# A two-layer hybrid decoder trunk: the prologue's modulation blocks in halves, its rotary sines moved behind its last split, and the last norm turned token-major by TensorE

## The chip, the cores and the metric

The kernel runs on one core of one Trainium2 chip. The metric is the time of one execution on the device in microseconds (us), the median of several runs. Three runs of the kernel before gave 935.73, 937.77 and 939.75 us.

## The reference

Two layers over 256 tokens of width 1024, in float32. Each layer forms six modulation vectors from the conditioning vector `c`, runs three attention branches side by side from one input projection, and then an MLP. Only the start and the end matter here:

```python
c_act = jax.nn.silu(c)
for l in range(DEPTH):
    mod = c_act @ w_ada[l] + b_ada[l]                 # w_ada[l]: 1024 x 6144
    shift1, scale1, gate1, shift2, scale2, gate2 = jnp.split(mod, 6, axis=-1)
    hdn = modulate(rmsnorm(x, norm1_g[l]), shift1, scale1)
    proj = hdn @ w_in[l]
    q_lat, c_kv, k_pe, sb_qkv, mb_qkv, gates = jnp.split(proj, SPLIT_POINTS, axis=-1)
    ...                                               # MLA, stick-breaking and MoBA attention
    x = x + gate1[:, None, :] * (merged @ w_out[l])
    hdn = modulate(rmsnorm(x, norm2_g[l]), shift2, scale2)
    x = x + gate2[:, None, :] * (jnp.square(jax.nn.relu(hdn @ w_ff1[l])) @ w_ff2[l])
return rmsnorm(x, final_norm_g)
```

`rmsnorm` divides by the root of the mean square over the 1024 channels, `modulate` is `h * (1 + scale) + shift`. The rotary embeddings of two branches need sines and cosines of the positions.

## The kernel before

The residual `x` lies with channels on the partitions: 8 tiles `x[:, k, :]` of 128 channels by 256 tokens. Weights are streamed in blocks of 1 MB by DMAs that SyncE (SP) issues. A block is a `Job`: `fetch` loads it into a tile `ws`, ScalarE (ACT) rounds it into `wh` and VectorE (DVE) forms the remainder `wl = ws - wh` (`split_piece`, four pieces to a job), and TensorE (PE) multiplies with three matmuls per product (`wh` by high part, `wh` by low part, `wl` by high part). The jobs stand in one list and are worked through in order.

The prologue is written out by hand and keeps its order on every engine. It computes `mod` of the first norm on DVE: `ada` multiplies a block of `w_ada` (two columns of 1024 numbers per partition) with the broadcast activated `c` in `cb` and sums along the row. Channel pairs q = 0 to 3 follow each other. For each pair, block 4 + q (the scale) and block q (the shift) are loaded as `adaw`, and then two jobs of the input projection (`ws`, jobs 2q and 2q + 1, cut into pieces of 256 KB). The pair's two channel tiles are scaled (`ht`) and shifted. For q = 0 and 1 TensorE multiplies them unsplit in float32 (`hf` by `ws`, "plain" jobs 0 to 3); for q = 2 and 3 they are split into `hh`, `hl` (tile `act`) and their weights (jobs 4 to 7) into `wh`, `wl`. All four pairs add up in the same PSUM banks (`first`). When the last pair is through, ACT copies the banks out to `sbqk`, from which the stick-breaking scores `z` are made; the `z` tiles take the same PSUM slots as the banks (tag "at", two slots). Then follow job 8 (tile `ps`, of the MoBA projection), jobs 9 and 10, and job 11, a further block of `w_ada`.

SP's queue holds DMAs back by semaphores: each waits for the one issued eight before it, and later ones for the `ws` slot that they fill (three slots).

`table_angles` reduces the rotary angles on DVE and `tables` takes their absolute value and sines on ACT, which loads another function table and loads the old one back. `warm` issues matmuls that nobody reads.

At the end, `x_last` adds the last two channel tiles, `Rms.sum` adds the squares over channels on PE, `Rms.root` forms the reciprocal root for a 128 x 256 tile, and four DVE products make the output, still with channels on the partitions, in four DMAs.

Of the kernel before, what the change touches and what calls it, by code (L numbers as in the profile page):

```python
# [20 lines left out]
D = 1024  # L21
# [14 lines left out]
WARM = 12, 2, 20  # L36
# [4 lines left out]
def trunk(ctx, tc, xT, heads, pos, signs, masks, gfin, wada, win, wkpe, wuq, wukv, wo, wout, wff1, wff2, out):  # L41
# [56 lines left out]
    def table_angles():  # L98
        row = t256("row")
        nc.vector.tensor_copy(row[0:1, :], posi)  # L100
        posf = mmps("posf")[:, 0, :]
        nc.tensor.matmul(posf, minus[0:1, :], row[0:1, :], start=True, stop=True)
        c1 = 6.28125
# [7 lines left out]
        nc.vector.tensor_scalar(n, n, MAGIC, None, op0=OP.subtract)  # L111
        for f in (c1, c2, c3):
            nc.vector.scalar_tensor_tensor(ang, n, -f, ang, op0=OP.mult, op1=OP.add)
        nc.vector.tensor_scalar(ang, ang, PI_SAFE, -PI_SAFE, op0=OP.min, op1=OP.max)

# [23 lines left out]
    class Job:  # L139
        def __init__(self, src, f, parts, raw=False, plain=None, mms=24):  # L140
            self.src, self.f, self.parts, self.raw, self.plain, self.mms = src, f, parts, raw, plain, mms

# [276 lines left out]
    def first_jobs(qk_done, sbv, start):  # L419
# [12 lines left out]
        def part(u, i, o, q):  # L432
            def go(wh, wl):
                ps = bank(u)
                ks = range(2 * q, 2 * q + 2)
# [11 lines left out]
                else:  # L447
                    v_part(ps, i, wh, wl, o, ks, q < PLAIN_Q)
# [8 lines left out]
        for q in range(4):  # L457
            for us, tag in ((range(4), "wh"), (range(4, 6), "wl")):
                jobs.append(Job([win[0, u][:, q * 512:q * 512 + 512] for u in us], 512 * len(us),
                                [part(u, i, 512 * (u - us[0]), q) for u in us for i in range(2)],  # L460
                                plain=tag if q < PLAIN_Q else None))
# [126 lines left out]
    def layer(l):  # L588
# [244 lines left out]
        def x_last(i, ps, sec):  # L833
# [5 lines left out]
            if i == 0:  # L839
                go()  # L840
            else:
                rms["last"] = go
# [19 lines left out]
        def seam(then, n):  # L862
            def go():
                drain()
                tc.no_sync_barrier()
                with tc.manual_schedule():
# [3 lines left out]
                    else:  # L870
                        rms["last"]()
                        rms["q"].sum()
                        r = rms["q"].root()
                        for u in range(4):
                            o = t512("out")
                            nc.vector.tensor_mul(o, rms["xg"][:, 2 * u:2 * u + 2, :], bc(r))
                            nc.sync.dma_start(out[:, 2 * u:2 * u + 2, :], o)
                tc.no_sync_barrier()
                rest()
            return go  # L880

# [106 lines left out]
    with tc.manual_schedule():  # L988
# [19 lines left out]
        fetch_to(6)  # L1008
# [21 lines left out]
        table_angles()  # L1030
        warm(WARM[1])
        rq = Rms(D)
        for u in range(4):
# [3 lines left out]
        ada(0, 4, first_ada[4])  # L1037
        gs0 = gain(0, 48, 1, (0, 2))
        r = rq.root(scalar=True)
        nc.gpsimd.dma_start(csr, signs)  # L1040
        hf.append(work.tile([128, 4, S], F32, name="hf", tag="v", bufs=2))

        def start_job(i):
            split_to(i, PIECES)
            for part in jobs[i].parts:
                part(jobs[i].wh, jobs[i].wl)
# [6 lines left out]
        for q in range(4):  # L1053
            ks = range(2 * q, 2 * q + 2)
            if q:
                ada(0, 4 + q, first_ada[4 + q])
                gain(0, 48, 1, (2 * q, 2 * q + 2), gs0)
            if q < PLAIN_Q:
                ts = [scaled(k) for k in ks]
                ada(0, q, first_ada[q])  # L1060
                for k, t in zip(ks, ts):
                    nc.scalar.activation(hf[0][:, k, :], t, AF.Identity, bias=col(0, 0, k))
            else:
                ada(0, q, first_ada[q])
                if q < 3:
                    split_to(2 * q, 1)
                modulate(0, r, gs0, 0, ks)
            if q < 3:
                start_job(2 * q)
                start_job(2 * q + 1)  # L1070
                if q == 0:
                    tables()
                if q == 2:
                    fetch_to(7)
        split_to(6, PIECES)
        split_to(7, PIECES)
        for k in range(2 * PLAIN_Q):
            split(hh[:, k, :], hl[:, k, :], hf[0][:, k, :])
        state["auto"] = True
        fetch_to(7 + WS)  # L1080
# [99 lines left out]
```

## Time and profile before

| | before |
|---|---|
| median of 3 runs | 937.77 us (935.73 to 939.75) |
| profiled execution, its own time | 938.25 us |
| span in the profile | 936.5 us, 19142 instructions |
| PE busy | 915.7 us (98%) |
| DVE busy | 730.5 us (78%) |
| ACT busy | 599.1 us (64%) |
| DMA, mean over the span | 223 GB/s |
| granted TensorE clock, mean | 0.995 |

The span is the time between the first and the last thing that the profiler saw on the core; the execution's own time is 1.75 us longer. A PE that is busy 98% of the span leaves some 20 us in which it waits, and those lie in the first 90 us, at two places in the middle and behind the last matmul. PE's busy time is modelled, so the waits are better read from when an instruction starts than from the sum.

### The profile page before, as it was taken

How to read it: one execution, taken by the hardware profiler on the slowest of the kernel's cores; microseconds unless marked ns; L12 is line 12 of the kernel's file. 1: busy time of each engine (PE TensorE's matmuls, PEld its weight loads, DVE VectorE, ACT ScalarE, POOL GpSimd, SP SyncE). 2: the span in 40 equal slices, each digit the busy share in tenths (PEclk: the TensorE clock that was granted, in tenths of full speed). 3: DMA queues.
4: the chain of work that ended last, by engine and by line, in shares of the span. 5: the costliest groups of instructions: out<-in, count | busy, mean ns of one | idle time of the engine just before them, and what ended most of it. 6: DMA issues, size and time to landing. Idle time of an engine off the chain costs nothing.

```text
span 936.5 us, 19142 instructions
## 1 busy us (share of the span) xinstructions
PE 915.7 (98%) x7771; PEld 889.6 (95%) x7772; DVE 730.5 (78%) x1414; ACT 599.1 (64%) x1251; POOL 9.6 (1%) x15
## 2 busy tenths in 40 slices
PE   7998999999999999999999999999999999999996
PEld 4998999899999999999999999989999999999995
DVE  6878788887799976767897978879787989554554
ACT  4277678867576874645576677886677677563641
POOL 0000000000000000000000000000000000000012
PEclk9999999999999999999999999999999999999998
DMA  9956564565657388677847554645666647755531
GB/s 339 386 205 231 185 225 159 214 235 196 245 225 270 140 310 305 236 270 266 324 174 274 222 203 155 229 169 210 240 221 228 212 150 284 256 181 190 186 121 45
DMA packets 32634, 208.77 MB, mean 223 GB/s; under 512 B 3745, under 2 KB 4130, under 8 KB 8994
## 3 DMA queue, kind: packets, MB, share of 16 engines
q1 hardware_dynamic: 32400, 207.35, 61.7%
q8 instruction: 61, 1.00, 0.4%
q0 software_dynamic: 144, 0.20, 0.1%
q14 instruction: 27, 0.22, 0.1%
q10 hardware_dynamic: 2, 0.00, 0.0%
HBM read 206.49 MB, written 1.05 MB: 222 GB/s over the span
## 4 chain that ended last, share of the span: by engine, by line
PE 84%; DVE 6%; DMA 6%; ACT 2%; issue 1%; SPq 0%; DVEq 0%; ACTq 0%
PE ps L342 17%; PE ps L343 16%; PE ps L344 16%; PE ff L939 5%; PE ff L942 5%; PE ff L940 5%; DMA ws<-win 5%; PE pre L364 4%; DVE wl L178 3%; PE po L469 1%; DMA ws<-wada 1%; PE vps L342 1%; PE vps L344 1%; PE vps L343 1%; PE s L524 1%; PE z L510 1%
## 5 line engine op out<-in xcount | busy, mean ns | idle before, releaser
L178 DVE TENSOR_TENSOR wl<-ws,wh 128x512 fp32r<-128x512 f32 (+1 forms) x592 | 378.7, 675 | 128.6 <-ACT wh L177 128.0
L177 ACT ACTIVATE wh<-ws 128x512 fp32r<-128x512 f32 (+1 forms) x592 | 336.8, 615 | 208.2 <-PE ps L343 97.3
L342 PE MATMUL ps<-act,wh 128*128 128x256 f32 x1120 | 312.0, 279 | 0.0
L344 PE MATMUL ps<-act,wl 128*128 128x256 f32 x1120 | 310.3, 277 | 0.0
L343 PE MATMUL ps<-act,wh 128*128 128x256 f32 x1120 | 310.1, 277 | 0.0
L342 PEld LDWEIGHTS ps<-act,wh 128*128 128x128 f32 x1120 | 210.4, 188 | 0.5 <-DVE wl L178 0.3
L344 PEld LDWEIGHTS ps<-act,wl 128*128 128x128 f32 x1120 | 210.9, 188 | 0.0
L343 PEld LDWEIGHTS ps<-act,wh 128*128 128x128 f32 x1120 | 210.4, 188 | 0.2
L939 PE MATMUL ff<-fh,wh 128*128 128x256 f32 x448 | 123.6, 276 | 0.0
L940 PE MATMUL ff<-fl,wh 128*128 128x256 f32 x448 | 123.6, 276 | 0.0
L942 PE MATMUL ff<-fh,wl 128*128 128x256 f32 x448 | 123.6, 276 | 0.0
L242 DVE SCALAR_TENSOR_TENSOR ws<-ws,cb 128x1024 f32<-128x1024 f32 x80 | 95.9, 1221 | 22.5 <-DMA ws<-wada 22.1
L939 PEld LDWEIGHTS ff<-fh,wh 128*128 128x128 f32 x448 | 84.1, 188 | 0.0
L940 PEld LDWEIGHTS ff<-fl,wh 128*128 128x128 f32 x448 | 84.1, 188 | 0.0
L942 PEld LDWEIGHTS ff<-fh,wl 128*128 128x128 f32 x448 | 84.1, 188 | 0.0
L544 ACT ACTIVATE e<-s,st 128x128 f32<-128x128 f32 (+1 forms) x64 | 26.0, 432 | 23.6 <-DVE st L539 23.6
L364 PE MATMUL pre<-xh,wh 128*128 128x258 f32 x96 | 28.3, 295 | 0.0
L364 PE MATMUL pre<-xh,wl 128*128 128x258 f32 x96 | 27.1, 283 | 0.0
L364 PE MATMUL pre<-xl,wh 128*128 128x258 f32 x96 | 27.1, 282 | 0.0
L342 PE MATMUL vps<-wh,act 128*128 128x256 f32 x96 | 26.9, 280 | 0.0
L343 PE MATMUL vps<-wl,act 128*128 128x256 f32 x96 | 26.7, 278 | 0.0
L344 PE MATMUL vps<-wh,act 128*128 128x256 f32 x96 | 26.7, 278 | 0.0
(259 smaller groups left out, 1738.6 us busy)
## 6 DMA issues: line engine op xcount, KB each, us to landing
ws<-wff SPq DMA_DIRECT2D x64, 1024.0 KB, 4.9
ws<-win SPq DMA_DIRECT2D x50, 1024.0 KB, 4.9
ws<-wada SPq DMA_DIRECT2D x40, 1024.0 KB, 4.9
ws<-wo SPq DMA_DIRECT2D x12, 1024.0 KB, 4.9
adaw<-wada SPq DMA_DIRECT2D x8, 1024.0 KB, 9.2
ws<-wout SPq DMA_DIRECT2D x8, 1024.0 KB, 4.9
ws<-win SPq DMA_DIRECT2D x24, 256.0 KB, 9.1
ws<-wuq SPq DMA_DIRECT2D x6, 768.0 KB, 4.3
```

The costliest lines, as they stand in the source:

```text
L177: nc.scalar.activation(job.wh[:, a], job.ws[:, a], AF.Copy)
L178: nc.vector.tensor_sub(job.wl[:, a], job.ws[:, a], job.wh[:, a].bitcast(F32))
L242: nc.vector.scalar_tensor_tensor(w, w, 1.0, cb, op0=OP.mult, op1=OP.mult, accum_out=mods[l][:, 2 * b + i:2 * b + i + 1])
L342: nc.tensor.matmul(o, wh, ah, start=first, stop=False)
L343: nc.tensor.matmul(o, wh, al, start=False, stop=False)
L344: nc.tensor.matmul(o, wl, ah, start=False, stop=last)
L364: nc.tensor.matmul(ps[:, i, 0:258], w[:, c:c + 128], a[:, k, :], start=k == 0 and n == 0, stop=k == KT - 1 and n == 2, skip_group_check=True)
L469: nc.tensor.matmul(po[64 * h:64 * h + 64, u, o:256], v[:, k, vc:vc + 64], pT[:, h, c:c + n], start=k == 0, stop=k == 1, tile_position=(0, ...
L544: nc.scalar.activation(e[:, h, a:b], s[:, h, a:b], AF.Exp, scale=scale, bias=st[:, 4 + c:5 + c], accum_out=st[:, 8 + c:9 + c])
L939: nc.tensor.matmul(o, wh[:, c0:c0 + 128], fh[:, k, :], start=st, stop=False, skip_group_check=True)
L940: nc.tensor.matmul(o, wh[:, c0:c0 + 128], fl[:, k, :], start=False, stop=False, skip_group_check=True)
L942: nc.tensor.matmul(o, wl[:, c0:c0 + 128], fh[:, k, :], start=False, stop=en, skip_group_check=True)
```

## The change

In the prologue each block of `w_ada` is loaded in two halves of 512 KB, in the order scale, shift, scale, shift, and each half is worked off by itself (`ada_col`: product and sum, then one 128 x 1 operation). The first two channel tiles are modulated one at a time, and the first group of matmuls goes over the channel tile k outermost. One pair of squares moves from ACT to DVE. The angles' reduction is cut in three: the position matmul stays, the first four operations stand behind the first pair's modulation, and the last four, with the sines on ACT, stand behind the last splits of the prologue. Jobs 6 and 7 load into spare slots, so that job 8 can be fetched earlier. Fewer warm matmuls are issued. In pairs 2 and 3 the first piece of the weight split stands between the two low parts of the activations.

At the end, the products with the gain are turned by TensorE transposes to tokens on the partitions, the sums of squares are made for tokens on the partitions (128 x 2), the root is taken of 128 x 2 numbers, and ACT and DVE copy the turned tiles out with the root as a scale, in three pieces each, with six DMAs.

```diff
-WARM = 12, 2, 20
+WARM = 7, 2, 14
...
     def fetch(i):
         job = jobs[i]
-        job.ws = wpool.tile([128, 2048], F32, name="ws", tag=job.plain or "ws", bufs=WB if job.plain else WS)
+        if job.spare:
+            job.ws = slot("ws").rearrange("p a b -> p (a b)")
+        else:
+            job.ws = wpool.tile([128, 2048], F32, name="ws", tag=job.plain or "ws", bufs=WB if job.plain else WS)
...
+        def tail():
+            q, xg = rms["q"], rms["xg"]
+            ft = [atps(f"ft{t}") for t in range(2)]
+            ts = mmps("tsum")
...
+            total([q.acc] + q.late, True, False)
+            q.late = []
+            turn(range(1))
+            x_one(7, rms["end"], 5)
+            q.square_late(x[:, 7, :])
+            nc.vector.tensor_scalar(xg[:, 7, :], x[:, 7, :], gf[:, 7:8], None, op0=OP.mult)
+            total(q.late, False, True)
+            turn(range(1, KT))
...
+            for a, b in ((0, 256), (256, 512), (512, 1024)):
+                h, c = a // 512, slice(a % 512, a % 512 + b - a)
+                nc.scalar.activation(os[0][h][:, c], ft[0][:, h, c], AF.Copy, scale=r[:, 0:1])
+                nc.vector.tensor_scalar(os[1][h][:, c], ft[1][:, h, c], r[:, 1:2], None, op0=OP.mult)
+                for t, e in ((0, nc.scalar if h else nc.sync), (1, nc.sync)):
+                    e.dma_start(out[toks[t], a:b], os[t][h][:, c])
...
             for b in (4 + q, q):
-                t = slot("adaw").rearrange("p a b -> p (a b)")
-                nc.sync.dma_start(t, wada[0, b])
-                first_ada[b] = t
+                first_ada[b] = slot("adaw").rearrange("p a b -> p (a b)")
+            for i in range(2):
+                for b in (4 + q, q):
+                    nc.sync.dma_start(first_ada[b][:, i * D:i * D + D], wada[0, b][:, i * D:i * D + D])
...
+        def ada_col(b, i):
+            w = first_ada[b][:, i * D:i * D + D]
+            c = slice(2 * b + i, 2 * b + i + 1)
+            m = mods[0][:, c]
+            nc.vector.scalar_tensor_tensor(w, w, 1.0, cb, op0=OP.mult, op1=OP.mult, accum_out=m)
+            if b < 4:
+                nc.vector.tensor_add(m, m, vec[:, 0, c])
+            else:
+                k = 2 * (b - 4) + i
+                nc.vector.scalar_tensor_tensor(gs0[:, k:k + 1], m, onep[:, k:k + 1], vec[:, 0, 48 + k:49 + k],
+                                               op0=OP.add, op1=OP.mult)
...
+        ada_col(4, 0)
+        ada_col(0, 0)
+        r = rq.root(scalar=True)
...
+        plain_act(0, scaled(0))
+        ada_col(4, 1)
+        ada_col(0, 1)
+        plain_act(1, scaled(1))
+        next(angles)
+        split_to(1, PIECES)
+        for k in range(2):
+            for i in range(2):
+                start_job(i, [k])
...
+        for q in (2, 3):
+            k = 2 * q
+            ada_col(4 + q, 0)
+            ada_col(q, 0)
+            ta = scaled(k)
+            high(k, ta)
+            ada_col(4 + q, 1)
+            low(k, ta)
+            ada_col(q, 1)
+            tb = scaled(k + 1)
+            high(k + 1, tb)
+            split_to(2 * q, 1)
+            low(k + 1, tb)
...
         split_to(6, PIECES)
         split_to(7, PIECES)
         for k in range(2 * PLAIN_Q):
             split(hh[:, k, :], hl[:, k, :], hf[0][:, k, :])
+        next(angles)
+        tables()
         state["auto"] = True
-        fetch_to(7 + WS)
```

What this does to the order on the engines is shown at three places. The first is ScalarE at the end of the prologue: `wh` are the rounded weights of jobs 6 and 7 (four pieces each) and then of job 8, `act<-hf` the splits of the plain activations, `sbqk<-first` the copies out of the PSUM banks. Before:

```order
L335 ACTIVATE act<-ht,mod 128x256 x2
L177 ACTIVATE wh<-ws 128x512 x4
L177 ACTIVATE wh<-ws 128x256 x4
L234 ACTIVATE act<-hf 128x256 x4
L177 ACTIVATE wh<-ws 128x512 x4
L596 ACTIVATE sbqk<-first 128x256
```

The same place in the changed kernel, where `tab` is the tile of the rotary tables:

```order
L184 ACTIVATE wh<-ws 128x512 x4
L184 ACTIVATE wh<-ws 128x256 x4
L241 ACTIVATE act<-hf 128x256 x4
L121 ACTIVATE tab<-tab 128x512
L122 ACT_TABLE_LOAD
L122 ACTIVATE tab<-tab 128x512
L123 ACTIVATE tab<-tab,quarter 128x512
L124 ACT_TABLE_LOAD
L184 ACTIVATE wh<-ws 128x512 x4
L603 ACTIVATE sbqk<-first 128x256
```

The five instructions on `tab`, which stood before behind the first `hf` pair, now stand between the last splits and the weights of job 8, and ahead of the copies to `sbqk`.

The second place is VectorE at the same point of the program. Before (`act<-hf` are the low parts of the plain activations, the five `wl` those of job 8 and one piece of job 9, `ws<-ws,cb` job 11's block of `w_ada`):

```order
L334 SCALAR_TENSOR_TENSOR ht<-x,gs_233,rr 128x256 x2
L338 SCALAR_TENSOR_TENSOR act<-ht,mod_90,act 128x256 x2
L178 TENSOR_TENSOR wl<-ws,wh 128x512 x4
L178 TENSOR_TENSOR wl<-ws,wh 128x256 x4
L235 TENSOR_TENSOR act<-hf,act 128x256 x4
L178 TENSOR_TENSOR wl<-ws,wh 128x512 x5
L242 SCALAR_TENSOR_TENSOR ws,mod_90<-ws,cb 128x1024 x2
```

In the changed kernel, from the last scaled tile on:

```order
L1107 SCALAR_TENSOR_TENSOR ht<-x,gs_226,rr 128x256
L185 TENSOR_TENSOR wl<-ws,wh 128x512
L1117 SCALAR_TENSOR_TENSOR act<-ht,mod_90,act 128x256
L185 TENSOR_TENSOR wl<-ws,wh 128x512 x3
L185 TENSOR_TENSOR wl<-ws,wh 128x256 x4
L242 TENSOR_TENSOR act<-hf,act 128x256 x4
L115 SCALAR_TENSOR_TENSOR tab<-tab 128x512 x3
L116 TENSOR_SCALAR tab<-tab 128x512
L185 TENSOR_TENSOR wl<-ws,wh 128x512 x5
L249 SCALAR_TENSOR_TENSOR ws,mod_90<-ws,cb 128x1024
```

One piece of the weight split now stands between the two low parts of the activations, and four operations on the angles stand ahead of job 8's pieces.

The third place is VectorE at the first channel pair, from the position's cast on. Before:

```order
L100 CAST row<-posi 1x256
L109 TENSOR_SCALAR tab<-posf,head 128x256 x2
L110 TENSOR_SCALAR tab<-tab 128x512
L111 TENSOR_SCALAR tab<-tab 128x512
L113 SCALAR_TENSOR_TENSOR tab<-tab 128x512 x3
L114 TENSOR_SCALAR tab<-tab 128x512
L242 SCALAR_TENSOR_TENSOR adaw,mod_90<-adaw,cb 128x1024 x2
L247 TENSOR_TENSOR mod_90<-mod_90,head 128x2
L325 SCALAR_TENSOR_TENSOR gs_233<-mod_90,head 128x2
L313 TENSOR_TENSOR v<-v,y_237 128x256
L315 SCALAR_TENSOR_TENSOR rr<-v,yh 128x256
L1050 SCALAR_TENSOR_TENSOR ht<-x,gs_233,rr 128x256 x2
```

In the changed kernel:

```order
L100 CAST row<-posi 1x256
L1083 TENSOR_TENSOR sq<-x 128x256 x2
L1084 TENSOR_TENSOR sq<-sq 128x256
L1097 SCALAR_TENSOR_TENSOR adaw,mod_90<-adaw,cb 128x1024
L1102 SCALAR_TENSOR_TENSOR gs_226<-mod_90,onep,head 128x1
L1097 SCALAR_TENSOR_TENSOR adaw,mod_90<-adaw,cb 128x1024
L1099 TENSOR_TENSOR mod_90<-mod_90,head 128x1
L320 TENSOR_TENSOR v<-v,y_233 128x256
L322 SCALAR_TENSOR_TENSOR rr<-v,yh 128x256
L1107 SCALAR_TENSOR_TENSOR ht<-x,gs_226,rr 128x256
```

All work on the angles left the front of the first block, two squares came to VectorE, and the first scaled tile needs two halves in place of a whole block.

## Rows read from the trace of the kernel before

**Rows 1.** Waits of PE: who waited for whom, us in total, times, longest.

```profile
PE first L441 <- ACT hf L1062: 3.1, 1, 3.1
```

**Rows 2.** Stretches: busy us per engine (instructions), granted clock, DMA share, GB/s.

```profile
25.00:30.00 5.00, 5.00 (x25) 4.41 (x24) 1.70 (x5) 0.91 (x2) 0.00 (x0) 1.00 1.00 412
```

**Rows 3.** DVE's timeline: start, length (us), line, operation, idle before.

```profile
30.05 1.23 DVE L242 SCALAR_TENSOR_TENSOR adaw<-adaw,cb 128x1024 f32<-128x1024 f32 x1 [3.32 <-DMA adaw<-wada]
...
32.74 1.22 DVE L242 SCALAR_TENSOR_TENSOR adaw<-adaw,cb 128x1024 f32<-128x1024 f32 x1
...
47.18 0.89 DVE L338 SCALAR_TENSOR_TENSOR act<-ht,mod,act 128x256 fp32r<-128x256 f32 x2 [0.18 <-ACT act L335]
48.10 3.84 DVE L178 TENSOR_TENSOR wl<-ws,wh 128x512 fp32r<-128x512 f32 x8
51.86 1.42 DVE L235 TENSOR_TENSOR act<-hf,act 128x256 fp32r<-128x256 f32 x4
53.20 2.49 DVE L178 TENSOR_TENSOR wl<-ws,wh 128x512 fp32r<-128x512 f32 x4
```

**Rows 4.** ACT's timeline at the end of the prologue.

```profile
50.76 1.33 ACT L234 ACTIVATE act<-hf 128x256 fp32r<-128x256 f32 x4
51.99 2.19 ACT L177 ACTIVATE wh<-ws 128x512 fp32r<-128x512 f32 x4
54.08 0.37 ACT L596 ACTIVATE sbqk<-first 128x256 f32<-128x256 f32 x1
```

**Rows 5.** DVE's timeline on the rotary angles.

```profile
10.12 2.15 DVE L113 SCALAR_TENSOR_TENSOR tab<-tab 128x512 f32<-128x512 f32 x3
12.30 0.43 DVE L114 TENSOR_SCALAR tab<-tab 128x512 f32<-128x512 f32 x1
```

**Rows 6.** ACT's timeline on the rotary sines: the first and the last of five.

```profile
20.52 0.61 ACT L118 ACTIVATE tab<-tab 128x512 f32<-128x512 f32 x1
...
23.70 1.28 ACT L121 ACT_TABLE_LOAD   x1
```

**Rows 7.** PE's timeline from the first scores to job 8.

```profile
57.84 0.70 PE L478 MATMUL z<-sbqk 64*128 64x256 f32 x4
...
58.60 0.60 PE L478 MATMUL z<-sbqk 64*128 64x256 f32 x4
...
59.79 0.36 PE L342 MATMUL ps<-act,wh 128*128 128x256 f32 x1
```

**Rows 8.** Stretches behind the prologue and behind one wait of layer 1.

```profile
70.00:75.00 5.00, 3.98 (x35) 3.76 (x34) 2.98 (x5) 4.62 (x8) 0.00 (x0) 1.00 0.92 360
75.00:80.00 5.00, 3.75 (x25) 3.31 (x24) 5.00 (x9) 5.00 (x11) 0.00 (x0) 1.00 0.15 31
85.00:90.00 5.00, 4.36 (x42) 3.96 (x40) 4.96 (x11) 2.00 (x4) 0.00 (x0) 1.00 0.87 326
619.00:623.00 4.00, 4.00 (x15) 3.21 (x14) 1.82 (x5) 2.85 (x7) 0.00 (x0) 0.57 0.61 188
```

**Rows 9.** DVE's timeline at job 11's block of `w_ada` and behind it.

```profile
62.77 1.22 DVE L242 SCALAR_TENSOR_TENSOR ws<-ws,cb 128x1024 f32<-128x1024 f32 x1 [5.87 <-DMA ws<-wada]
...
69.36 0.95 DVE L500 SCALAR_TENSOR_TENSOR l<-z,l 128x768 f32<-128x768 f32 x1
```

**Rows 10.** Issues of DMAs of the whole span: count, size, median us to landing.

```profile
ws<-wada SPq DMA_DIRECT2D x40, 1024.0 KB, 4.9
```

**Rows 11.** Timeline of the end, all engines.

```profile
926.36 0.48 DVE L799 SCALAR_TENSOR_TENSOR x<-xl,mod,x 128x256 f32<-128x256 f32 x1 [2.24 <-PE xl L942]
...
927.34 0.70 PE L299 MATMUL ssum<-sql,negs 128*128 128x256 f32 x2 [0.16 <-ACT sql L291]
...
930.55 2.50 DVE L876 TENSOR_TENSOR out<-xg,rr 128x512 f32<-128x512 f32 x4
931.26 2.14 SPq L877 DMA_DIRECT2D outT<-out  x4
```

**Rows 12.** PE's timeline at one group of transposes.

```profile
137.96 1.48 PE L560 MATMUL pt<-head,e 128*128 128x128 f32 x12
```

More of the change, by code (lines that the diff above doesn't have):

```diff
@@ L841, in x_last @@
             else:
-                rms["last"] = go
+                rms["last"], rms["end"] = go, ps
         def wout_done(u):
@@ L870, in go @@
                     else:
[L871 to L877, printed above, removed]
+                        tail()
                 tc.no_sync_barrier()
@@ L1007, in trunk @@
         ada_fetch(3)
-        fetch_to(6)
+        fetch_to(8)
         nc.sync.dma_start(msk, masks)
@@ L1029, in trunk @@
             nc.scalar.activation(cb[:, 512 * h:512 * h + 512], cps[:, h, :], AF.Copy)
-        table_angles()
+        onep = cpool.tile([128, KT], F32, name="onep")
+        nc.vector.tensor_scalar(onep, vec[:, 0, 8:16], 1.0, None, op0=OP.add)
+        angles = table_angles()
+        next(angles)
         warm(WARM[1])
         rq = Rms(D)
-        for u in range(4):
+        sqa = t512("sq")
+        for k in range(2):
+            nc.vector.tensor_mul(sqa[:, k, :], x[:, k, :], x[:, k, :])
+        nc.vector.tensor_add(sqa[:, 0, :], sqa[:, 0, :], sqa[:, 1, :])
+        rq.late.append(sqa[:, 0, :])
+        for u in range(1, 4):
             rq.square(*x_pair(u), keep=True)
@@ L1036, in trunk @@
         warm(WARM[2])
[L1037 to L1046, printed above, removed]
+        gs0 = cpool.tile([128, KT], F32, name="gs00")
+        first_ht = {}
+        def ada_col(b, i):
[9 more added lines that the diff above has]
+                                               op0=OP.add, op1=OP.mult)
         def scaled(k):
@@ L1051, in scaled, with plain_act @@
             return t
[L1053 to L1074, printed above, removed]
+        def plain_act(k, t):
+            nc.scalar.activation(hf[0][:, k, :], t, AF.Identity, bias=col(0, 0, k))
@@ new lines, in high, with low, start_job @@
+        def high(k, t):
+            nc.scalar.activation(hh[:, k, :], t, AF.Identity, bias=col(0, 0, k))
+        def low(k, t):
+            nc.vector.scalar_tensor_tensor(hl[:, k, :], t, col(0, 0, k), hh[:, k, :].bitcast(F32),
+                                           op0=OP.add, op1=OP.subtract)
+        def start_job(i, ks=None):
+            split_to(i, PIECES)
+            for part in jobs[i].parts:
+                part(jobs[i].wh, jobs[i].wl, ks)
+        ada_col(4, 0)
+        ada_col(0, 0)
@@ new lines, in trunk @@
+        r = rq.root(scalar=True)
+        nc.gpsimd.dma_start(csr, signs)
+        hf.append(work.tile([128, 4, S], F32, name="hf", tag="v", bufs=2))
+        plain_act(0, scaled(0))
[4 more added lines that the diff above has]
+        split_to(1, PIECES)
+        for k in range(2):
+            for i in range(2):
+                start_job(i, [k])
+        for i in range(2):
+            ada_col(5, i)
+            ada_col(1, i)
+            plain_act(2 + i, scaled(2 + i))
@@ new lines, in trunk @@
+        start_job(2)
+        start_job(3)
+        for q in (2, 3):
[11 more added lines that the diff above has]
+            low(k + 1, tb)
+            if q == 2:
+                for i in (4, 5):
+                    start_job(i)
+                    fetch_to(i + 5)
@@ L1078, in trunk @@
             split(hh[:, k, :], hl[:, k, :], hf[0][:, k, :])
+        next(angles)
+        tables()
         state["auto"] = True
-        fetch_to(7 + WS)
     tc.no_sync_barrier()
```

40 lines of the change are left out of this document (32 added, 8 removed).

## The prediction, on record before the changed kernel ran

> **What bounds the kernel now.** I read first who TensorE waits for, then what the stretches move, then the timelines of VectorE and ScalarE at the places found.
>
> TensorE's one long wait in the prologue is 3.1 us, for the first modulated tile [rows 1]. That invites an earlier start, and most of the change works on it. But an earlier first matmul pays only if what follows also comes earlier. From 25 to 30 us the 16 DMA engines are busy all the time at 412 GB/s, while VectorE works 1.70 of 5 us [rows 2]. VectorE then stands 3.32 us until block 6 of the modulation weights lands at 30.05 [rows 3]. So the third channel pair is paced by the stream of weights, and no reordering ahead of it makes that block land earlier; its first half can come earlier by half a block.
>
> Behind 30.05 VectorE is full to the end of the prologue: the two activation splits start at 47.18, the weight splits of jobs 6 and 7 at 48.10, the low parts of the plain activations at 51.86, job 8's split at 53.20, with a wait of 0.18 us among them [rows 3]. ScalarE ends its last prologue work at 51.99, rounds job 8's weights and copies the banks out from 54.08 on [rows 4]. TensorE takes the first scores at 57.84, the second at 58.60, job 8 at 59.79 [rows 7]. The order that counts is therefore: VectorE's chain from block 6, then ScalarE's copies, then the scores, which share PSUM slots with the banks and stand ahead of job 8 on TensorE.
>
> **The change, step by step.** All times are those of the profiled execution, 938.25 us with a span of 936.5.
>
> Start of the third pair. Half a block is 0.52 MB, at 412 GB/s 1.27 us [rows 2]. VectorE starts at 28.78 instead of 30.05 [rows 3]. Bytes and their order up to there stay the same.
>
> What rows 2 show is a full stream, whatever the size of a transfer. The Trainium skill (DMA: Bandwidth & Descriptors, section Bandwidth) says to batch transfers to at least 1 MiB, and its fit gives each some 2 us of fixed cost; by that rule the eight more transfers would cost, as an estimate, up to 16 us if they ran one by one. The trace's full stream, with transfers of 256 KB among them, does not bear that out.
>
> VectorE on pairs 2 and 3. Each pair has four small operations where there were three, and each waits for the sum just before it. Two columns with their two small operations take 2.69 us now, 30.05 to 32.74 [rows 3]; bounds for the addition are 0 and 0.5 us per pair, I take 0.2, since most of the operations exist already. Worse, a piece of the weight split now stands between the two low parts. It needs ScalarE to pass the scaled tile (like a copy of 128 x 256, 0.37 us [rows 4]) and to round a piece (128 x 512, like the 0.61 us [rows 6]), so VectorE stands about 1.0 us where it stood 0.18: 0.8 more per pair (0 if a piece were rounded ahead; it is not, ScalarE's row order has it behind). The low parts of the plain activations thus end at 53.20 - 1.27 + 0.4 + 1.6 = 53.93.
>
> The angles. The four operations that move behind them take 10.12 to 12.73, 2.61 us [rows 5]: 56.54. Before, they lay where VectorE waited for weights anyway.
>
> The sines. ScalarE has been idle since its own splits and waits for the angles. The block runs from 20.52 to 24.98, 4.46 us [rows 6]: 61.0. It stood where ScalarE had nothing to do; now job 8's weights and the copies out of the banks queue behind it. Three passes of about 0.6 and two table loads of 1.28 us fill these 4.46 us [rows 6]. The Trainium skill (ScalarE: Activation LUTs, section What ACT_TABLE_LOAD costs) puts a switch at 2.66 us, half of it a drain; by that the block would cost, as an estimate, 2.8 us more. The rows leave no room for a drain.
>
> Copies and scores. Job 8's four pieces take 54.08 - 51.99 = 2.09 us [rows 4]: 63.1. Four copies, one more piece, four copies follow: copies of 0.37 us overlap, so four take 1.05 to 1.5 us, I take 1.05; with a piece of 0.52 the second scores can start at 65.75, against 58.60: **+7.15 us** for TensorE. It will have stood since the end of the last pair, about 57.5, since an earlier first group cannot run ahead of the third pair's data. All that TensorE gains at the start is lost there, and so the finer first group, the moved squares and the fewer warm matmuls cost and bring nothing; their cover is this wait.
>
> What is late next. Job 11's load waits for job 8's split, which ended at 53.20 + 2.49 = 55.69 [rows 3] and now ends at about 63.95 (ScalarE's 63.1, a subtraction behind). With 4.9 us to landing [rows 10], the link being empty, VectorE gets it at 68.85 instead of 62.77, and the softplus term `l` behind it starts 6.1 us later than 69.36 [rows 9]. On that chain TensorE waits 2.27 us between 70 and 80 and 0.64 us between 85 and 90 [rows 8]. TensorE arrives 7.15 us late, the chain 6.1: about 1 us of these waits goes, and **+6.1 us** remain. Bounds: all 2.9 us of the waits absorbed, +4.3. Or the clock: after a wait the granted clock stood at a mean of 0.57 over 4 us in layer 1 [rows 8], 1.7 us lost, and a wait of six us may bring the same; if nothing absorbs it, +8.9. Behind 90 us TensorE is busy all but a few us, so what remains is not won back.
>
> The end. The last tile of `x` comes at 926.36 as before [rows 11]. The sums over tokens are four narrow matmuls behind the last square; 0.70 us is what the wide ones took [rows 11], I take 0.5: 927.85. Fourteen transposes follow, and twelve took 1.48 us in layer 0 [rows 12]; at 0.11 us each they end at 929.4. The root on 128 x 2 numbers is hidden behind them. Three copies per engine, like two pieces of 0.37 and one of 0.61 us with the PSUM read on top, take 1.5 us: 930.9, where the last product ended at 933.05 [rows 11]. Five of the six issues are SP's, at a quarter to half a us each [rows 11]: the last at 931.4 instead of 933.07, which gives 1.7 us. But the same 1.05 MB have to go out, 2.5 us at the 412 GB/s of rows 2, and from the first issue at 931.26 to the end of the span at 936.5 passed 5.24 us; from a first issue at 929.9 the same 5.24 lead to 935.1, which gives 1.4. I take **-1.3 us**; bounds 0 (transposes twice as slow) and -2.1 (all that the last copy gains).
>
> Sum: 938.25 + 6.1 - 1.3 = 943.05. The median shown is 0.5 us lower than the profiled execution and the runs spread over 4 us; I name **943.0 us**, 0.56% above the median. About 0.5%, 4.7 us, is what a measurement of this kernel can tell from no change: 933.1 to 942.5 counts as the same.
>
> **The rivals.**
>
> The early start is kept (faster). If the chain from block 6 were not what decides, TensorE would start earlier by the two columns left out (2.7 us [rows 3]) and the angles' 2.6 us [rows 5], 5.3 in all, and keep it: 938.25 - 5.3 - 1.3 = 931.7. For it speaks that TensorE's own wait list names only the first tile [rows 1]; against it the 3.32 us at 30.05 [rows 3]. It decides if ScalarE's sines are through by 52.0, where it took up job 8 before: 9 us earlier than worked out, more than that whole wait. Chance 0.11.
>
> The sines stay hidden (same). If the angles came early enough that ScalarE did them while TensorE is in the last pair, nothing moves there and the end alone counts: 936.9. It needs the block to end by 54, 7 us earlier. Or all waits to 90 us are absorbed and the end gives its best: 938.25 + 4.3 - 2.1 = 940.4. The first has a chance of 0.11; the second is the forecast's lower end.
>
> The halves slow the stream (slower). If it ran at the 360 GB/s of 70 to 75 us [rows 8] and not at 412, the 9 MB ahead of block 6's half would take 25.2 and not 22.0 us: 3.2 us more, 946.2. Rows 2 speak against it. Chance 0.05. (The Trainium skill's batching rule in DMA: Bandwidth & Descriptors, above, points this way.)
>
> **How the numbers follow.** The forecast has 0.73, its own range is 940.4 to 947.2 (8.9 and no gain at the end). Its centre lies just above the border of 942.5, so I put 0.45 above and 0.28 below it. Slower: 0.45 + 0.05 = 0.50. Same: 0.28 + 0.11 = 0.39. Faster: 0.11. A range from 937.5 to 947.0 holds the forecast but for its far end, the stream's case and part of the hidden sines, and leaves out the kept start: about 0.8.
>
> **What will show it.** In the changed profile TensorE's first group starts near 15 us, and TensorE stands for six us or so between 57 and 66 with ScalarE's copies as the releaser. VectorE's first column of block 6 starts near 28.8, the angles' last operation ends near 56.5, the second table load near 61, job 8 starts near 67. Job 11's columns start near 69. At the end the last output is issued about 5 us behind the last update of `x`. I am wrong if job 8 starts before 62, if VectorE has no wait ahead of block 6, or if the end takes as long as before.

## The result and the profile after

| | before | changed |
|---|---|---|
| median of 10 runs each, same chip | 938.64 us | 944.05 us |
| ratio, with its 95% interval | | 1.0072 (1.0051 to 1.0093) |
| profiled execution, own time / span | 938.25 / 936.5 us | 943.68 / 941.9 us |
| PE, DVE, ACT busy | 915.7, 730.5, 599.1 us | 920.3, 731.9, 599.0 us |

The ratio is estimated from all runs; the two medians alone give 1.0058. The changed kernel is slower by 0.6 to 0.7%, as forecast (943.0 us, slower as the likeliest of the three).

PE's list of waits in the changed kernel (total, times, longest) has a new head: the scores `z` wait for ScalarE's copies.

```profile
PE z L485 <- ACT sbqk L604: 5.1, 1, 5.1
PE first L448 <- ACT wh L184: 3.3, 2, 2.9
PE mvps L349 <- DVE gate L137: 3.0, 2, 1.5
```

VectorE's timeline, from block 6's first column on:

```profile
29.02 1.22 DVE L1097 SCALAR_TENSOR_TENSOR adaw<-adaw,cb 128x1024 f32<-128x1024 f32 x1 [3.34 <-DMA adaw<-wada]
...
36.89 0.69 DVE L185 TENSOR_TENSOR wl<-ws,wh 128x512 fp32r<-128x512 f32 x1 [1.09 <-ACT wh L184]
...
48.88 0.69 DVE L185 TENSOR_TENSOR wl<-ws,wh 128x512 fp32r<-128x512 f32 x1 [1.09 <-ACT wh L184]
...
53.03 1.43 DVE L242 TENSOR_TENSOR act<-hf,act 128x256 fp32r<-128x256 f32 x4
54.38 2.14 DVE L115 SCALAR_TENSOR_TENSOR tab<-tab 128x512 f32<-128x512 f32 x3
56.55 0.43 DVE L116 TENSOR_SCALAR tab<-tab 128x512 f32<-128x512 f32 x1
62.17 2.50 DVE L185 TENSOR_TENSOR wl<-ws,wh 128x512 fp32r<-128x512 f32 x4 [5.20 <-ACT wh L184]
...
69.55 1.23 DVE L249 SCALAR_TENSOR_TENSOR ws<-ws,cb 128x1024 f32<-128x1024 f32 x1 [3.52 <-DMA ws<-wada]
...
76.26 0.96 DVE L507 SCALAR_TENSOR_TENSOR l<-z,l 128x768 f32<-128x768 f32 x1
```

Against [rows 3] block 6 starts 1.03 us earlier. Two waits of 1.09 us at the split piece are new, then come the angles, then 5.20 us of standing for job 8's rounded weights. Job 11's column comes 6.78 us later than in [rows 9]. ScalarE's timeline shows what VectorE stood for:

```profile
51.54 1.32 ACT L241 ACTIVATE act<-hf 128x256 fp32r<-128x256 f32 x4
57.01 0.63 ACT L121 ACTIVATE tab<-tab 128x512 f32<-128x512 f32 x1 [4.15 <-DVE tab L116]
57.66 1.28 ACT L122 ACT_TABLE_LOAD   x1
58.95 0.63 ACT L122 ACTIVATE tab<-tab 128x512 f32<-128x512 f32 x1
...
60.22 1.28 ACT L124 ACT_TABLE_LOAD   x1
61.51 2.19 ACT L184 ACTIVATE wh<-ws 128x512 fp32r<-128x512 f32 x4
...
65.97 0.43 ACT L604 ACTIVATE sbqk<-first 128x256 f32<-128x256 f32 x1
```

ScalarE takes job 8's weights up at 61.51, where [rows 4] have 51.99: 4.15 us of waiting for the angles and 4.5 us of sines lie ahead of them. PE's timeline of the scores and job 8 (to compare with [rows 7]), then stretches with the granted clock as the last number but two:

```profile
64.84 1.23 PE L485 MATMUL z<-sbqk 64*128 64x256 f32 x4 [5.14 <-ACT sbqk L604]
...
66.46 1.22 PE L485 MATMUL z<-sbqk 64*128 64x256 f32 x4
...
68.83 0.56 PE L349 MATMUL ps<-act,wh 128*128 128x256 f32 x1
```

```profile
64.00:66.00 2.00, 1.16 (x6) 0.99 (x8) 1.33 (x3) 2.00 (x8) 0.00 (x0) 0.50 0.41 57
66.00:68.00 2.00, 2.00 (x14) 1.38 (x10) 0.03 (x1) 2.00 (x6) 0.00 (x0) 0.50 0.79 319
68.00:70.00 2.00, 2.00 (x15) 1.96 (x14) 0.45 (x1) 2.00 (x5) 0.00 (x0) 0.50 0.35 147
70.00:75.00 5.00, 5.00 (x45) 5.00 (x44) 5.00 (x10) 3.41 (x5) 0.00 (x0) 0.98 0.30 70
75.00:80.00 5.00, 5.00 (x46) 5.00 (x46) 3.14 (x5) 2.72 (x4) 0.00 (x0) 1.00 1.01 423
85.00:90.00 5.00, 5.00 (x41) 4.92 (x41) 5.00 (x10) 3.61 (x7) 0.00 (x0) 1.00 0.62 211
```

Behind its wait TensorE runs at the lower of its two levels, 1.2 GHz, to 70 us; a group of scores takes 1.23 us where it took 0.70. Job 8 is 9.04 us late, but the waits of 70 to 90 us in [rows 8] are gone. The end, all engines:

```profile
932.66 0.48 DVE L806 SCALAR_TENSOR_TENSOR x<-xl,mod,x 128x256 f32<-128x256 f32 x1 [2.24 <-PE xl L986]
...
933.65 0.61 PE L897 MATMUL tsum<-negs,sql 128*128 128x2 f32 x4
...
934.12 1.72 PE L892 MATMUL ft<-head,xg 128*128 128x128 f32 x14
...
935.88 1.54 DVE L922 TENSOR_SCALAR out<-ft,st 128x256 f32<-128x256 f32 x3 [0.43 <-PE ft L892]
936.27 2.43 SPq L924 DMA_DIRECT2D outT<-out  x5
937.22 0.37 ACTq L924 DMA_DIRECT2D outT<-out  x1
```

The last update of `x` comes 6.30 us later than in [rows 11], and from it to the end of the span pass 9.24 us instead of 10.14. The difference of the spans, 5.4 us, is 6.30 - 0.90.

### The profile page after: what moved, and what is told of

The parts are those of the page before. It is cut to its first block, busy times and chain, and to the rows that moved or that the text cites. A ratio compares the mean times of both kernels' runs of the same rounds, so it can differ in the third digit from the quotient of the medians.

```text
span 941.9 us, 19180 instructions
## 1 busy us (share of the span) xinstructions
PE 920.3 (98%) x7780; PEld 894.6 (95%) x7781; DVE 731.9 (78%) x1423; ACT 599.0 (64%) x1251; POOL 8.7 (1%) x14
## 4 chain that ended last, share of the span: by engine, by line
PE 79%; DVE 10%; DMA 5%; ACT 4%; issue 1%; SPq 0%; DVEq 0%; ACTq 0%
PE ps L349 15%; PE ps L350 15%; PE ps L351 15%; PE ff L983 5%; PE ff L984 5%; PE ff L986 5%; DVE wl L185 4%; PE pre L371 4%; DMA ws<-win 2%; DMA adaw<-wada 2%; PE po L476 1%; PE vps L349 1%; PE vps L350 1%; PE vps L351 1%; ACT wh L184 1%; DMA ws<-wada 1%
## 5 line engine op out<-in xcount | busy, mean ns | idle before, releaser
L350 PE MATMUL ps<-ml,wh 128*128 128x256 f32 x96 | 26.8, 282 | 0.6 <-DVE ml L242 0.6
L349 PE MATMUL vps<-wh,act 128*128 128x256 f32 x96 | 26.9, 280 | 0.0
L349 PE MATMUL ps<-mh,wh 128*128 128x256 f32 x96 | 26.6, 280 | 0.2 <-ACT mh L241 0.2
```

The source lines that it names most:

```text
L349: nc.tensor.matmul(o, wh, ah, start=first, stop=False)
L350: nc.tensor.matmul(o, wh, al, start=False, stop=False)
```

## Experiments

The theory: what counts is when ScalarE gets to job 8's weights, because the load of job 11 and with it VectorE's chain hang on them; TensorE's own start counts less. The rivals: the halves, the half clock, or the new end cost the time. The table has four moments of each profiled execution (us) and the timed ratio to the kernel before: TensorE's start of job 8, VectorE's first column of job 11, the first row maxima of the MoBA softmax, the last update of `x`.

| kernel | job 8 | job 11 | row maxima | last `x` | ratio (95% interval) |
|---|---|---|---|---|---|
| before | 59.79 | 62.77 | 123.00 | 926.36 | |
| changed | 68.83 | 69.55 | 130.03 | 932.66 | 1.0072 (1.0051 to 1.0093) |
| 1 before, sines last | 66.80 | 67.78 | 127.86 | 932.09 | 1.0067 (1.0046 to 1.0087) |
| 2 sines in the gap | 62.43 | 61.54 | 122.08 | 925.08 | 0.9970 (0.9955 to 0.9985) |
| 3 before, new end | 63.17 | 61.02 | 122.65 | 929.24 | 0.9984 (0.9964 to 1.0004) |
| 4 fill of 44 | 68.20 | 71.41 | 132.98 | 939.30 | 1.0087 (1.0059 to 1.0114) |
| 5 angles early, sines last | 63.13 | 64.95 | 125.15 | 927.12 | 0.9999 (0.9987 to 1.0011) |
| 6 gap, piece ahead | 59.08 | 59.79 | 120.20 | 923.56 | 0.9942 (0.9924 to 0.9959) |
| 7 sines at the old place | 62.87 | 64.50 | 124.78 | 926.87 | 0.9996 (0.9984 to 1.0007) |
| 8 fill of 40 | 67.69 | 71.06 | 132.64 | 935.50 | 1.0066 (1.0051 to 1.0081) |
| 9 as 2, first wait filled | 63.98 | 62.11 | 123.63 | 925.88 | 0.9990 (0.9972 to 1.0009) |
| 10 as 6, first wait filled | 66.02 | 62.62 | 125.67 | 929.28 | 0.9998 (0.9974 to 1.0023) |
| 11 as 2, filled again | 60.18 | 61.87 | 121.84 | 924.43 | 0.9986 (0.9967 to 1.0004) |
| 12 as 6, filled again | 57.98 | 60.12 | 120.22 | 922.34 | 0.9987 (0.9960 to 1.0014) |

The four moments are those of one execution each. Run 3 shows how far two executions of one order lie apart: up to its end it has the order of the kernel before on every engine, and yet job 8 comes 3.38 us later, job 11 1.75 earlier, the row maxima 0.35 earlier and the last `x` 2.88 later. A difference of less than some 3 us at the last `x` is therefore no effect by itself; the timed ratio has to show it.

**1. The kernel before with nothing but the sines last.**

```diff
 # kernel before, end of the prologue
             split(hh[:, k, :], hl[:, k, :], hf[0][:, k, :])
+        next(angles)
+        tables()
```

The call of `tables()` behind the first pair goes, and `table_angles()` pauses ahead of its last four operations. The order of everything else stays, but for the second column of job 11 on VectorE, which seven pieces of weight splits overtake.

> The kernel before with one edit: the angles' last four VectorE operations and the sines on ScalarE stand behind the last splits of the prologue; transfers, matmul order and end stay as before. Theory (the sines queue ahead of job 8's weights and the copies out of the banks): the copies to sbqk begin near 63, TensorE stands some five to six us ahead of the second scores, job 8 starts near 67 to 68.5 instead of 59.79, the last update of x comes 5 to 6.5 us later than 926.36, ratio 1.0055 to 1.007. Rival 1 (the halved transfers and the split-up columns cost the time): nothing of this, ratio 0.998 to 1.002. Rival 2 (the lower clock behind the wait is most of it): job 8 starts late, but the last update of x less than 3 us late.

TensorE's wait came with the same releaser:

```profile
63.02 1.23 PE L480 MATMUL z<-sbqk 64*128 64x256 f32 x4 [5.87 <-ACT sbqk L599]
```

The last `x` comes 5.73 us late against 6.30 in the full change, the row maxima 4.86 against 7.03, and the timed ratio is 1.0067 against 1.0072: this one move is enough for a loss of that size, and neither halves nor end are needed for it. Rival 1 falls by the ratio, rival 2 by the last `x`.

**2. The changed kernel with the sines where VectorE waits for weights.**

```diff
             plain_act(2 + i, scaled(2 + i))
+        next(angles)
+        tables()
         start_job(2)
...
-        next(angles)
-        tables()
```

> The changed kernel with one edit: the angles' last four operations and the sines stand directly behind the second pair's modulation, where VectorE waits 3.34 us for block 6 and ScalarE 6.07 us. Theory: ScalarE's second table load ends near 33, the low parts of the plain activations end near 54.4 as in the changed kernel, the copies to sbqk are held by TensorE alone, job 8 starts near 61 to 62 instead of 68.83, the last update of x falls from 932.66 to about 926.5 to 927.5; with the new end the ratio to before is 0.998 to 1.001. Rival 1 (halves and columns cost it): the last update of x stays above 930, ratio 1.004 or more. Rival 2 (the clock behind the wait): as the theory if the wait goes, since the wait is gone; not told apart here.

The order of everything else is that of the changed kernel, but for the second column of job 11 on VectorE, which now stands directly behind the first. The kernel gains 7.58 us at the last `x` and is faster than both kernels by the timed ratio. That is more than expected, though job 8 came later than expected (62.43).

**3. The kernel before with nothing but the new end** (the function `tail` and the new output layout).

> The kernel before with the new end alone (token-major last norm, transposes, six output DMAs). Theory: from the last update of x to the end of the span 9.24 us as in the changed kernel, instead of 10.14; ratio 0.9985 to 0.9995, below what timing can tell surely. Rival (the transposes and ScalarE's copies compete with work ahead of them once the prologue does not push them): no gain, 10.0 us or more.

From the last `x` to the end of the span pass 9.26 us, as in the changed kernel, 0.9 less than before. The timed ratio does not tell this from nothing.

**4 and 8. TensorE's wait filled, 44 and 40 matmuls.**

```diff
         def start_sb():
+            if l == 0:
+                wz = msps("wz")
+                wb = msk[:, 0:2, :].rearrange("p a b -> p (a b)")
+                for _ in range(FILL):
+                    nc.tensor.matmul(wz[:, 0:256], ident_b, wb, start=True, stop=True)
```

> The changed kernel with 44 bf16 matmuls of 256 columns that nobody reads in TensorE's wait ahead of the first scores; nothing else moves. Theory: the granted clock stays at 1.00 through 64 to 70, the scores take half the time, job 8 starts near 67 instead of 68.83, but the chain on job 11 (VectorE at 69.5, the softplus term at 76.3) is unchanged, TensorE waits for it between 80 and 92 instead, and the last update of x falls by less than 1 us (931.7 to 932.7); ratio 1.006 to 1.0075. Rival 2 (the lower clock is a cost of its own): the last update of x falls by 1.8 us or more, ratio 1.005 or less.

> The fill of TensorE's gap again, with 40 matmuls of 256 bf16 columns where 44 were: with 44 the order of the instructions behind the scores came out another one on every engine, with 40 it stays that of the changed kernel but for a few neighbours on VectorE and ScalarE. The added matmuls compute nothing that is read. The fill lasts from 58.6 to about 63.2; the scores then run at the full clock and job 8 starts 1.1 to 1.7 us earlier than at 68.83. Theory (job 11's block decides and swallows TensorE's lag): the last update of x stays at 932.2 to 933.2, ratio 1.006 to 1.008. Rival (the half clock behind the wait is a cost that is kept to the end): 931.0 or earlier, ratio 1.005.

Both misses. The clock did stay full (1.00 from 62 to 70 us), and with 40 job 8 came 1.14 us earlier; yet the last `x` came 6.6 and 2.8 us later than in the changed kernel, the row maxima 2.95 and 2.61. The second expectation also rests on an error of mine: the two fills change the order in the same few places. In the run with 40, PE's list and VectorE's timeline show where the start that was won ends (`rp` is a rotary product, `lh` the high part of the softplus term `l`):

```profile
PE rp L590 <- ACT lh L242: 2.7, 1, 2.7
```

```profile
71.06 1.23 DVE L250 SCALAR_TENSOR_TENSOR ws<-ws,cb 128x1024 f32<-128x1024 f32 x1 [5.08 <-DMA ws<-wada]
```

Job 11's block was issued at 64.65 (64.70 in the changed kernel) and taken up 1.51 us later than there; 1.14 early and 1.51 late make the new wait of 2.7 us. Behind it the clock fell again in both runs (0.50 from 86 to 88 us). It is VectorE's side that decides, but the changed neighbours and this second drop keep the two from being a clean test of the clock; 11 and 12 are cleaner.

**5. Angles early, sines last.** As 2, but `tables()` stays at the end.

> The changed kernel with the angles' last four operations back behind the second pair's modulation, where VectorE waits for weights; the sines and both table loads stay last on ScalarE. This takes away ScalarE's wait of 4.15 us for the angles and leaves the block of 4.46 us. Theory (what counts is when ScalarE comes to job 8's weights): the block begins at about 52.9 and ends at 57.4 instead of 61.5, the second scores can start 4.1 us earlier, job 11's block of w_ada lands at about 65.4 instead of 69.55, and the last update of x comes at 928.5 (928.0 to 929.3) instead of 932.66; ratio to the kernel before 1.002 to 1.004. Rival 1 (only the wait for the angles hurt, the sines are harmless): as with the sines in the gap, 925.1 and 0.997. Rival 2 (VectorE's angles never counted, since something else holds job 8): 932.7 and 1.007.

ScalarE's block runs from 52.41 to 56.88, job 11 comes 4.60 us earlier than in the changed kernel, the row maxima 4.88. So 4.6 to 4.9 us of the loss at these places came from the angles being late; against 2 some 3.1 to 3.4 us are left for the sines and loads. The last `x` and the ratio lie below the expected bands. Of the 5.54 us that the last `x` gained, 0.66 lie behind the row maxima, within the spread of run 3; why the timed ratio is lower too stays open.

**6. Sines in the gap, and the first weight piece rounded ahead.**

```diff
# on top of the edit of 2
...
             tb = scaled(k + 1)
-            high(k + 1, tb)
             split_to(2 * q, 1)
+            high(k + 1, tb)
             low(k + 1, tb)
```

> The changed kernel with the angles and sines behind the second pair's modulation, and in pairs 3 and 4 the first weight piece rounded by ScalarE ahead of the last scaled tile, so that VectorE has its piece ready. Theory (VectorE's chain from block 6 sets the end of the prologue): the two waits of 1.09 us go, the chain ends 2.2 us earlier, the last update of x comes at 922.9 to 923.5 instead of the 925.08 that the sines in the gap alone gave; ratio to the kernel before 0.994 to 0.996, faster than both kernels. Rival (the waits come back elsewhere: on ScalarE's rounding ahead of its own scaled tile, or on the stream, so that job 11's block lands no earlier): 924.5 to 925.5 and 0.997.

The two waits of 1.09 us are gone, job 11's load is issued 1.91 us earlier than in 2 (54.81 against 56.72) and taken up 1.75 us earlier. By its six runs this is the fastest kernel of the study: 933.96 us against 939.39 us of the kernel before on the same chip. Run 12, the same order with a fill, gave only 0.9987 on another chip, and the two intervals just fail to meet, so the size of this gain is not settled.

**7. All else of the change, angles and sines at their old place.**

> The changed kernel with all work on the angles and sines back at its place of before: angles ahead of the first half block, sines behind the first pair on ScalarE. All else, the halves, the first group by k and the new end, stays. Theory (the start ahead of block 6 is paced by the stream of weights, so an earlier first group is worth nothing): TensorE's first group starts 3 to 5 us later than in the changed kernel, VectorE still begins block 6 at about 29, and the last update of x comes where the sines in the gap put it, at 925.1 (924.6 to 925.6); ratio 0.997. Rival (the earlier start is worth something once the sines are out of the way): later by 1 us or more, 926 to 928, ratio 0.998 to 1.000.

A miss, and in the rival's band: 926.87 and 0.9996. TensorE's first group starts 8.17 us later than in the changed kernel (23.00 against 14.83), and job 11 is 2.96 us later than in 2. VectorE's timeline shows that it was not ready when block 6 landed:

```profile
11.74 0.76 DVE L1084 TENSOR_TENSOR sq<-x 128x256 f32<-128x256 f32 x2
...
20.93 0.43 DVE L320 TENSOR_TENSOR v<-v,y 128x256 f32<-128x256 f32 x1 [5.24 <-ACT y L318]
...
31.72 1.22 DVE L1098 SCALAR_TENSOR_TENSOR adaw<-adaw,cb 128x1024 f32<-128x1024 f32 x1
```

The squares that the change moved to VectorE stand here behind the angles, and TensorE waits for them before it sums them. Its sums of squares in the changed kernel, then in run 7, with the clock there:

```profile
7.76 3.34 PE L306 MATMUL ssum<-sq,negs 128*128 128x256 f32 x14
```

```profile
13.01 6.26 PE L306 MATMUL ssum<-sq,negs 128*128 128x256 f32 x14 [5.12 <-DVE sq L1085]
```

```profile
14.00:16.00 2.00, 2.00 (x6) 1.62 (x5) 1.62 (x6) 0.00 (x0) 0.00 (x0) 0.50 1.07 397
```

So the root is late twice over: the squares come late, and behind the wait the same fourteen matmuls take 2.92 us longer at the lower clock. Block 6 starts at 31.72 with no wait for it, 2.70 us later than in the changed kernel. Without the 2.92 us it would, as an estimate, have started at 28.80, ahead of the 29.02 at which the changed kernel had its weights. Here a lower clock on TensorE was passed on through VectorE.

**9 and 10. The wait ahead of pair 4 filled.** Between the third and the fourth pair, 22 matmuls in kernel 2, 20 in kernel 6:

```diff
+        wb = msk[:, 0:2, :].rearrange("p a b -> p (a b)")
...
                     fetch_to(i + 5)
+                wz = mmps("wz").rearrange("p a b -> p (a b)")
+                for _ in range(22):
+                    nc.tensor.matmul(wz[:, 0:256], ident_b, wb, start=True, stop=True)
```

> The kernel with the sines in the gap, and 22 matmuls of 256 bf16 columns that compute nothing that is read, put between the third and the fourth pair, where TensorE stands from 46.0 to 48.7 us and then works on pair 4 at half the clock until 55.6. The order on the engines stays but for the second column of job 11 on VectorE. If the wait is what drops the clock, pair 4 runs at the full clock and ends about 3 us earlier: first scores at 57.3 to 58.0 instead of 60.49, job 8 at 59.3 to 60.0 instead of 62.43. Theory (job 11's block on VectorE, which does not move, decides behind the prologue): little of it arrives, the last update of x comes at 924.0 to 925.0 instead of 925.08, and TensorE shows new waits between 70 and 90 us. Rival (the half clock is a cost that is kept): 922.0 to 922.8 and a ratio of 0.994 where the sines in the gap gave 0.997.

> The kernel with the sines in the gap and the first weight piece rounded ahead, with 20 such matmuls between the third and the fourth pair, where TensorE waits 1.96 us and then works at half the clock for about 3.5 us. Theory (job 11's block decides): job 8 comes 1 to 1.7 us earlier than at 59.08, the last update of x at 923.2 to 923.7 instead of 923.56, ratio 0.993 to 0.995. Rival (the half clock is kept): 921.9 to 922.5, ratio 0.992 to 0.993.

Inconclusive on the clock: the fill reads the masks, whose load stands late in SP's queue. It waited 3.4 and 4.6 us for them and then delayed pair 4. What the delay did shows in the table: in 9 job 8 and the row maxima both come 1.55 us later than in 2.

**11 and 12. The same fill from a tile that is there** (`ident_b` and `wb` replaced by parts of `wsrc`).

> The fill between the third and the fourth pair once more, now with the signs tile as its operand, which has been there since the start; the masks tile of the runs before landed at 49.6 us only, so that the fill waited and then ran into pair 4. 22 matmuls of 256 bf16 columns, base is the kernel with the sines in the gap; the order of everything else is the same on every engine. The fill lasts from 46.0 to 48.6, pair 4 runs at the full clock, first scores at 57.3 to 58.0 instead of 60.49, job 8 at 59.3 to 60.0 instead of 62.43. Theory (job 11's block on VectorE decides behind the prologue): the last update of x at 924.0 to 925.0 instead of 925.08, with new waits of TensorE between 70 and 90 us. Rival (the half clock is a cost that is kept): 922.0 to 922.8, ratio 0.994.

> The same fill, 20 matmuls, in the kernel with the sines in the gap and the piece rounded ahead; the order of everything else is that of this kernel. The fill lasts from 44.7 to 47.0, and pair 4 runs at the full clock, where it ran at half of it from 47.4 to 50.5. Theory (job 11's block decides): job 8 comes 1 to 1.7 us earlier than at 59.08, the last update of x at 923.2 to 923.7 instead of 923.56, ratio 0.993 to 0.995. Rival (the half clock is kept): 921.9 to 922.5, ratio 0.992 to 0.993.

Stretches of kernel 2, then of kernel 11, then the fill's row in PE's timeline of kernel 11:

```profile
49.00:51.00 2.00, 2.00 (x9) 1.77 (x10) 2.00 (x5) 2.00 (x6) 0.00 (x0) 0.50 1.01 422
53.00:55.00 2.00, 2.00 (x12) 2.00 (x11) 2.00 (x6) 2.00 (x6) 0.00 (x0) 0.50 0.01 4
```

```profile
49.00:51.00 2.00, 1.78 (x12) 1.47 (x13) 2.00 (x4) 2.00 (x6) 0.00 (x0) 1.00 0.97 406
53.00:55.00 2.00, 2.00 (x20) 2.00 (x19) 2.00 (x7) 2.00 (x5) 0.00 (x0) 1.00 0.01 4
75.00:80.00 5.00, 3.78 (x28) 3.39 (x27) 5.00 (x9) 4.87 (x9) 0.00 (x0) 1.00 0.20 43
```

```profile
46.16 2.58 PE L1167 MATMUL wz<-csr 128*128 128x256 bf16 x22
```

With the fill TensorE works on pair 4 at its full clock, 20 instead of 12 matmuls in two microseconds, and job 8 comes 2.25 us earlier. VectorE's job 11 does not move (61.87 against 61.54), TensorE waits 1.22 us from 75 to 80, and at the row maxima 0.24 us are left of 2.25. With kernel 6 as base, 1.10 us at job 8 leave nothing at the row maxima (120.22 against 120.20). That kernel's last `x` lies 1.22 us earlier all the same, in the rival's band; the table places that behind the row maxima, where the order is the same, and it is less than the 2.88 us of run 3. The timed ratio, 0.9987, lies in neither band and shows no gain over run 6.

## Why the prediction was right, step by step

The forecast of 943.0 us stands against 944.05, and its sum against the profiled execution: 938.25 + 6.30 - 0.90 = 943.65, measured 943.68. Its terms:

- *Start of the third pair.* 28.78 forecast, 29.02 measured. From 25 to 30 us the halves moved 407 GB/s where [rows 2] have 412, so the rival of the slowed stream falls, and the Trainium skill's batching rule that pointed its way (DMA: Bandwidth & Descriptors, Bandwidth) did not bind here.
- *VectorE on pairs 2 and 3* (the third and the fourth, counted from 0). A stand of 1.0 us per pair forecast, 1.09 measured; run 6 took both away, and job 11's load was issued 1.91 us earlier.
- *Angles and sines.* Ends 56.54 and 61.0 forecast, 56.98 and 61.50 measured; runs 1 and 2 show that this block is the loss. Each table load takes 1.28 us and the next operation starts 0.01 us behind it. The Trainium skill (ScalarE: Activation LUTs, What ACT_TABLE_LOAD costs) adds a drain to such a load and makes it 2.66 us per switch; this trace has the load but no room for the drain.
- *Job 8.* +7.15 us forecast, +9.04 measured. Mis-sized: the second scores were 0.71 us later, and from them to job 8 passed 2.37 us instead of 1.19, at half the clock. The forecast had the clock as a bound, not in the sum. It also missed a new wait of TensorE ahead of the fourth pair, 2.88 us for ScalarE's `wh`, with the lower clock behind it (0.50 from 50 to 53 us): the last pair ended at 59.70 and not near 57.5. Behind the sines this made no difference; in run 2 ScalarE waits 1.80 us for that pair.
- *Job 11 and `l`.* 68.85 and +6.1 us forecast, 69.55 and +6.9 measured. The load itself was issued 8.98 us later (64.70 against 55.72): from issue to VectorE's column it took 7.05 us in the profile of the kernel before, and 4.93 in run 3, which has the same order. The forecast set its 4.9 us for the changed kernel against that slow landing, so that this term has its size by some 2 us of luck.
- *What remains.* +6.1 us forecast, +6.30 measured, by two errors against each other: TensorE was later than thought, and the waits behind it took up more than the 1 us that I gave them. Those of 70 to 90 us are all gone, and that of `mvps` fell from 4.3 to 3.0 us. From job 8 to the row maxima TensorE waited 2.91 us in the kernel before and 0.30 in the changed one. Both chains are late there by about as much, since both hang on ScalarE, and which of them holds the row maxima is not shown. The bound of +8.9 ("if nothing absorbs it") was the wrong worry, as these waits were there to absorb it.
- *The end.* -1.3 us forecast, -0.9 measured. The first output is issued 3.61 us behind the last `x` (3.54 forecast); the mis-sized term is the way from there to the end, taken as 5.24 us from [rows 11], now 5.63.
- *"All that TensorE gains at the start is lost"*, and so the moves there bring nothing: right for the changed kernel, where the first group starts at 14.83 and PE stands at 64. As a rule it failed in run 7: with the halves VectorE has only 3.34 us to spare at block 6, and the late squares, with the 2.92 us that the lower clock added to their sums, used more.

Of the rivals, the kept early start and the hidden sines needed ScalarE at job 8 by 52 or 54; it came at 61.5.

The table says which chain paces the start: the one that is later. From job 11's column to the row maxima pass 59.97 to 60.54 us in nine kernels. In 3, 9 and 10 it is 61.5 to 63.1; there, and in 2, the row maxima follow job 8 by 59.48 to 59.65 us, and TensorE has no wait on the way. So kernel 2 stands between the two chains, which is why 2.25 us at job 8 were worth only 0.24 in run 11. Runs 4 and 8 fit neither, with 61.6 us from job 11 and 64.8 and 65.0 from job 8; there a fill changed neighbours in the order. Job 11's landing took 6.3 and 6.4 us from its issue in runs 4 and 8 and 7.05 in the kernel before, which has no fill, against 4.8 to 5.0 in the other kernels whose VectorE waited for it; why stays open.

## What to carry to other kernels

A block of work that leaves a place where its engine only waited for weights costs up to its full length where it lands (here 3.1 to 3.4 us of a block of 4.5), and the wait for its inputs on top (here 4.6 to 4.9): look at what is queued behind it on that engine, and whose load hangs on that. Find the chain that paces the stretch, here most often an in-order VectorE that stands for a weight block, before paying for an earlier start or a faster clock on the engine that is busiest. Once the chain is known the repair is small: the same sines in a gap made the slower kernel faster than the one before. And take two executions of one order before reading a small difference between two profiles.

## What the runs showed of the hardware

After a wait of 2.60 us (kernel 2, ahead of pair 4) the granted clock was 0.50 from 49 to 55 us; after 1.96 us (kernel 6) it was 0.50 from 48 to 50 us too. Not every such wait does this. At the same place run 4 waited 2.59 us and stayed at 1.00. Ahead of the first group the kernel before waited 3.13 us and run 3, with the same order, 3.12 us; the stretches behind these waits are, first of the kernel before, then of run 3:

```profile
20.00:25.00 5.00, 4.74 (x22) 4.14 (x23) 4.34 (x9) 4.94 (x7) 0.00 (x0) 1.00 1.07 393
```

```profile
20.00:25.00 5.00, 4.20 (x10) 3.39 (x11) 4.86 (x14) 4.71 (x7) 0.00 (x0) 0.50 1.08 391
```

With matmuls that nobody reads put into the wait ahead of pair 4 the clock was 1.00 in both runs, 11 and 12. That they kept it is likely but not shown, as run 4 kept it without them.

What the lower clock costs depends on who is late. In runs 11 and 12 the time won back was swallowed, as the theory on record had it, by TensorE's waits for VectorE between 70 and 80 us; in run 7 VectorE itself waited for the slow matmuls, and block 6 came 2.70 us late.
